# Pooling layer of a two-layer decoder: token scale moved from the tokens to the band matrices, bands built once, first squares split, GpSimd's weight parts in four pieces

## The chip, the cores and the metric

One core of a Trainium2 chip. Its engines run their own instruction queues side by side and wait for each other by semaphores: TensorE (PE in the rows, PEld for its weight loads), VectorE (DVE), ScalarE (ACT), GpSimd (POOL) and SyncE (SP), which here issues all DMAs. The metric is the device time of one launch in microseconds; lower is better.

## The reference

`x` has 512 tokens of 1024 channels, fp32. Layer 0 is a causal pooling mixer and an MLP, layer 1 sliding-window attention and an MLP; each sub-layer has a pre-RMSNorm and a residual, and a final norm follows. The change lies in the pooling mixer:

```
hn = rms_norm(x, g)                      # per token: x * rsqrt(mean(x*x) + eps) * g
for group g, window w in (2, 4, 8, 16):  # 256 channels each
    p_g = mean of hn over the last min(t, w) tokens - hn
y = einsum(p, w_pool) + b                # four 256 x 256 matrices
x = x + y * scale                        # then rms_norm, and the MLP
```

## The kernel before, in words

Activations lie transposed, with 128 channels on the partitions and 512 tokens along the row (eight tiles, `h[c]`). A large matrix product is done as three passes of a rounded 32-bit type: each operand is split in a high part `_h` (ScalarE, a copy that rounds) and a low part `_l` (the difference, on VectorE or GpSimd), and `mm3` (L84 to L86) adds high x high, high x low and low x high in PSUM.

The start of the program, up to about 30 us, is the pooling layer:

- SyncE loads four token tiles `xt` (128 tokens x 1024 channels), then `w_pool`, the small vectors `vec`, the first three weight tiles of the MLP (`wi_raw`, L90), then `h` (the transposed input).
- TensorE does twelve warm-up matmuls (L263) on zeros.
- GpSimd builds eight band matrices of 128 x 144 (L161 to L172): four windows, each once for the first tile (where the mean has fewer tokens) and once for the others. A band column holds 1/w on the tokens of the window, minus 1 on the token itself. A matmul of a token tile against a band gives pooled and transposed channels at once.
- For each token tile ScalarE squares it with a sum per token (L266), a square root, a reciprocal and one Newton step on VectorE give `r0`, VectorE multiplies the whole tile by it (L268, 128 x 1024), and eight fp32 matmuls (L271; each appears as two records) add into eight PSUM banks, one per 128 channels.
- ScalarE and GpSimd split `w_pool` (`wpool_h` L284, `wpool_l` L285). `px_h` (ScalarE, L251) and `px_l` (VectorE, L252) split the pooled banks; after each second one a tile of the MLP's weights is split (`in_weights`, L98 on ScalarE and L99 on GpSimd).
- 48 matmuls of L84 to L86 do the group matrices; `h` gets the result (L305); `f0x_h` and `f0x_l` split it for the MLP, whose first 96 matmuls follow. `n_sq` and `n_acc` (L215, L224 on GpSimd) sum the squares for the next norm, which is applied after these matmuls (L230, L241).

From there on the program is the MLP and the attention layer, with the same splitting. A scheduler puts the instructions of each engine into a fixed order at build time; each engine then works through its own list strictly in that order. The tile pools decide what must wait for a buffer.

## Time and profile before

| | us |
|---|---|
| median of 3 runs | 931.27 |
| the runs | 931.06, 931.27, 932.01 |
| the profiled execution | 932.39 |
| its span | 930.6 |

| engine | busy us | share |
|---|---|---|
| TensorE matmul | 915.2 | 98% |
| VectorE | 574.8 | 62% |
| ScalarE | 427.3 | 46% |
| GpSimd | 135.1 | 15% |

Every row of the trace is from the profiled execution; its times count from the span's start. A row of the timeline gives the start, the length, the engine, the source line and the operation, what it writes and reads, and how many like instructions are merged (x4). In brackets stands how long the engine was idle before it and what it waited for.

### The profile page before, as it was taken

Reading aid. Unit: us, or ns where it says so; the run is one execution under the profiler, and the core shown is the slowest. Engines: PE = TensorE matmul, PEld = TensorE weight load, DVE = VectorE, ACT = ScalarE, POOL = GpSimd, SP = SyncE. Lnnn points to the kernel's source line nnn. Section 1 sums busy time; section 2 is a strip of 40 time slices with the busy share of each in tenths; the row PEclk is TensorE's granted clock in tenths of the full one; section 3 lists DMA queues with packets and bytes.
Section 4 is the critical chain, followed back from the end, with each engine's and each line's share of the span. In section 5 each row is a group of like instructions: output and inputs, shape, how many; then the busy total and the mean of one; then the engine's idle time right before and its main releaser. Section 6 shows DMA issues by size and latency. Waiting matters only on the chain.

```text
span 930.6 us, 11682 instructions
## 1 busy us (share of the span) xinstructions
PE 915.2 (98%) x4419; PEld 771.5 (83%) x4419; DVE 574.8 (62%) x945; ACT 427.3 (46%) x690; POOL 135.1 (15%) x217
## 2 busy tenths in 40 slices
PE   8999999999999999999899999999999999999996
PEld 7788888888888888898788888888888888888896
DVE  5679766335777754456777482987743377777433
ACT  7655443223444443337787451644422244444532
POOL 9600000000000001325654140000000000000022
PEclk9999999999999999999999999999999999999999
DMA  9133222333223223322111041242233422322312
GB/s 333 67 113 113 93 84 80 93 128 113 91 91 105 65 87 106 114 91 68 50 43 46 2 158 39 98 139 104 63 93 100 136 91 91 111 80 63 95 60 91
DMA packets 28855, 88.13 MB, mean 95 GB/s; under 512 B 3200, under 2 KB 4352, under 8 KB 28800
## 3 DMA queue, kind: packets, MB, share of 16 engines
q1 hardware_dynamic: 28800, 87.40, 28.5%
q8 instruction: 34, 0.56, 0.2%
q14 instruction: 21, 0.17, 0.1%
HBM read 85.29 MB, written 2.10 MB: 94 GB/s over the span
## 4 chain that ended last, share of the span: by engine, by line
PE 92%; ACT 3%; DVE 2%; POOL 2%; issue 1%; POOLq 0%; ACTq 0%
PE bank L84 30%; PE bank L85 30%; PE bank L86 30%; PE bank L548 1%; PE bank L578 1%; ACT sc L565 1%; DVE q L464 1%; ACT px_h L251 0%; POOL sc L570 0%; PE bank L241 0%; ACT q_u L457 0%; DVE sc L551 0%; ACT wi_h L98 0%; PE bank L271 0%; ACT th L581 0%
## 5 line engine op out<-in xcount | busy, mean ns | idle before, releaser
L224 POOL TENSOR_TENSOR n_acc<-n_acc,n_sq 128x512 f32<-128x512 f32 (+1 forms) x28 | 39.1, 1395 | 716.4 <-ACT n_sq L215 709.8
L98 ACT ACTIVATE wi_h<-wi_raw 128x1024 fp32r<-128x1024 f32 x88 | 93.0, 1061 | 109.0 <-PE bank L85 100.5
L85 PE MATMUL bank<-f0x_l,wi_h 128*128 128x512 f32 x352 | 137.1, 389 | 0.8 <-DVE f0x_l L252 0.8
L84 PE MATMUL bank<-f0x_h,wi_h 128*128 128x512 f32 x352 | 137.3, 390 | 0.0
L84 PE MATMUL bank<-f1x_h,wi_h 128*128 128x512 f32 x352 | 137.2, 390 | 0.0
L84 PE MATMUL bank<-zh,wo_h 128*128 128x512 f32 (+1 forms) x363 | 137.1, 378 | 0.0
L86 PE MATMUL bank<-f0x_h,wi_l 128*128 128x512 f32 x352 | 137.0, 389 | 0.0
L86 PE MATMUL bank<-f1x_h,wi_l 128*128 128x512 f32 x352 | 137.0, 389 | 0.0
L85 PE MATMUL bank<-f1x_l,wi_h 128*128 128x512 f32 x352 | 137.0, 389 | 0.0
L86 PE MATMUL bank<-zh,wo_l 128*128 128x512 f32 (+1 forms) x363 | 136.6, 376 | 0.0
L85 PE MATMUL bank<-zl,wo_h 128*128 128x512 f32 (+1 forms) x363 | 136.6, 376 | 0.0
L99 DVE TENSOR_TENSOR wi_l<-wi_raw,wi_h 128x1024 fp32r<-128x1024 f32 x84 | 102.6, 1223 | 49.2 <-ACT wi_h L98 37.3
L98 ACT ACTIVATE wo_h<-wo_raw 128x768 fp32r<-128x768 f32 (+1 forms) x70 | 57.5, 823 | 120.2 <-PE bank L85 108.5
L313 DVE TENSOR_TENSOR c_u<-bank,n_rb 128x512 f32<-128x512 f32 x88 | 59.9, 687 | 75.9 <-PE bank L86 75.9
L99 DVE TENSOR_TENSOR wo_l<-wo_raw,wo_h 128x768 fp32r<-128x768 f32 (+1 forms) x66 | 60.3, 914 | 54.4 <-ACT wo_h L98 54.2
L86 PEld LDWEIGHTS bank<-zh,wo_l 128*128 128x128 f32 x363 | 68.3, 188 | 12.5
L84 PEld LDWEIGHTS bank<-zh,wo_h 128*128 128x128 f32 x363 | 68.3, 188 | 12.3
L85 PEld LDWEIGHTS bank<-zl,wo_h 128*128 128x128 f32 x363 | 68.3, 188 | 12.3
L85 PEld LDWEIGHTS bank<-f0x_l,wi_h 128*128 128x128 f32 x352 | 66.1, 188 | 14.6 <-DVE f0x_l L252 1.2
L84 PEld LDWEIGHTS bank<-f0x_h,wi_h 128*128 128x128 f32 x352 | 66.1, 188 | 14.2 <-DVE h L305 0.4
L86 PEld LDWEIGHTS bank<-f1x_h,wi_l 128*128 128x128 f32 x352 | 66.1, 188 | 13.9
L316 ACT ACTIVATE c_t<-c_u,vec 128x512 f32<-128x512 f32 x88 | 70.6, 811 | 15.3 <-DVE c_u L313 14.5
(173 smaller groups left out, 1488.7 us busy)
## 6 DMA issues: line engine op xcount, KB each, us to landing
wi_raw<-w_in SPq DMA_DIRECT2D x88, 512.0 KB, 3.2
wo_raw<-w_out SPq DMA_DIRECT2D x31, 384.0 KB, 3.0
wo_raw<-w_out SPq DMA_DIRECT2D x31, 320.0 KB, 2.8
kq_raw<-w_kq SPq DMA_DIRECT2D x10, 512.0 KB, 3.2
wo_raw<-w_o SPq DMA_DIRECT2D x8, 512.0 KB, 3.2
xt<-x_tok SPq DMA_DIRECT2D x4, 512.0 KB, 5.2
h<-x_t SPq DMA_DIRECT2D x8, 256.0 KB, 7.5
wpool_raw<-w_pool SPq DMA_DIRECT2D x2, 512.0 KB, 8.5
```

The source lines that it names most:

```text
L84: T.matmul(ps, lhsT=wh, rhs=xh, start=start, stop=False, **kw)
L85: T.matmul(ps, lhsT=wh, rhs=xl, start=False, stop=False, **kw)
L86: T.matmul(ps, lhsT=wl, rhs=xh, start=False, stop=stop, **kw)
L98: A.activation(h[:, :n], raw[:, :n], AF.Copy)
L99: (eng or V).tensor_tensor(l[:, :n], raw[:, :n], h[:, :n].bitcast(F32), ALU.subtract)
L224: eng.tensor_tensor(self.acc[:, lo:hi], self.acc[:, lo:hi], sq[:, lo:hi], ALU.add)
L313: V.tensor_tensor(u, ps, rb, ALU.mult)
L316: A.activation(t, u, AF.Identity, bias=col(V_CB + layer * 2 * NF + m), scale=cw[2])
L464: V.tensor_tensor(t[dst], u[src], t[src].bitcast(F32), ALU.subtract)
L548: T.matmul(o, lhsT=qt, rhs=kt[:, kk : kk + 256], start=x == 0, stop=x == 1)
L565: A.activation(t, t, AF.Exp, bias=neg[:, i : i + 1], scale=-1.0, accum_out=den[:, i : i + 1])
L578: T.transpose(ps[:, i * P : (i + 1) * P], sc[i // 2][:, i % 2, kb * P : (kb + 1) * P], ident)
```

## The change

Four bands are built on GpSimd and only the edge part of the other four; VectorE fills the rest by copies, and does the four memsets. The token scale is no longer multiplied into the token tile but into a copy of the band (`sband`, four instructions of 128 x 144 for each tile, two buffers in turn): the matmuls now take the raw tile and the scaled band. The square of the first tile is split in halves, one on ScalarE and one on VectorE, and the sums are added. The low parts that GpSimd makes of the first four MLP weight tiles are made in four instructions of 256 columns instead of one of 1024.

```diff
@@ weights, in_weights
-    def weights(src, n, name, eng=None, raw=None):
+    def weights(src, n, name, eng=None, raw=None, step=1024):
...
         A.activation(h[:, :n], raw[:, :n], AF.Copy)
-        (eng or V).tensor_tensor(l[:, :n], raw[:, :n], h[:, :n].bitcast(F32), ALU.subtract)
+        for a in range(0, n, step):
+            o = slice(a, min(a + step, n))
+            (eng or V).tensor_tensor(l[:, o], raw[:, o], h[:, o].bitcast(F32), ALU.subtract)
         return h, l
...
     def in_weights(layer, j, s, eng=None, raw=None):
-        return weights(w_in[layer, j, s], D, f"wi{layer}_{j}_{s}", eng, raw)
+        return weights(w_in[layer, j, s], D, f"wi{layer}_{j}_{s}", eng, raw, 256 if eng else 1024)
@@ the bands
-    for edge in (True, False):
-        for g, w in enumerate(WINDOWS):
-            b = band[:, 4 * edge + g, :]
-            G.memset(b, 1.0 / w)
-            G.affine_select(b, b, [[1, BW]], ALU.is_ge, 0.0, base=0, channel_multiplier=-1)
-            G.affine_select(b, b, [[-1, BW]], ALU.is_ge, 0.0, base=w - 1, channel_multiplier=1)
-            G.affine_select(b, b, [[1, BW]], ALU.not_equal, 1.0 / w - 1.0, base=0, channel_multiplier=-1)
-            if edge:
-                f = b[:, : w - 1]
-                G.affine_select(f, rc[:, : w - 1], [[1, w - 1]], ALU.is_ge, 0.0, base=0, channel_multiplier=-1)
-                G.tensor_tensor(f, f, ident[:, : w - 1], ALU.subtract)
+    for g, w in enumerate(WINDOWS):
+        b = band[:, g, :]
+        V.memset(b, 1.0 / w)
+        G.affine_select(b, b, [[1, BW]], ALU.is_ge, 0.0, base=0, channel_multiplier=-1)
+        G.affine_select(b, b, [[-1, BW]], ALU.is_ge, 0.0, base=w - 1, channel_multiplier=1)
+        G.affine_select(b, b, [[1, BW]], ALU.not_equal, 1.0 / w - 1.0, base=0, channel_multiplier=-1)
+        f = band[:, 4 + g, : w - 1]
+        G.affine_select(f, rc[:, : w - 1], [[1, w - 1]], ALU.is_ge, 0.0, base=0, channel_multiplier=-1)
+        G.tensor_tensor(f, f, ident[:, : w - 1], ALU.subtract)
+        V.tensor_copy(band[:, 4 + g, w - 1 :], b[:, w - 1 :])
@@ pool_mixer
-        ss0 = small(fst, NT, 32, name="ss0")
+        ss0 = small(fst, 2 * NT, 32, name="ss0")
...
         for i in range(NT):
+            cut = D // 2 if i == 0 else D
             junk = fst.tile([P, D], F32, tag="junk", name=f"junk{i}")
-            A.activation(junk, xt[:, i, :], AF.Square, accum_out=ss0[:, i : i + 1])
+            if cut < D:
+                V.tensor_tensor_reduce(
+                    out=junk[:, cut:], in0=xt[:, i, cut:], in1=xt[:, i, cut:], scale=1.0, scalar=0.0,
+                    op0=ALU.mult, op1=ALU.add, accum_out=ss0[:, NT : NT + 1],
+                )
+            A.activation(junk[:, :cut], xt[:, i, :cut], AF.Square, accum_out=ss0[:, i : i + 1])
+            if cut < D:
+                V.tensor_tensor(ss0[:, i : i + 1], ss0[:, i : i + 1], ss0[:, NT : NT + 1], ALU.add)
             rsqrt_mean(r0[:, i : i + 1], ss0[:, i : i + 1], 1, root=True)
-            V.tensor_scalar(xt[:, i, :], xt[:, i, :], r0[:, i : i + 1], None, ALU.mult)
             n = min(BW, S - i * P)
+            sband = fst.tile([P, 4, BW], F32, tag="sband", name=f"sband{i}", bufs=2)
+            for g in range(4):
+                V.tensor_scalar(sband[:, g, :n], band[:, (0 if i else 4) + g, :n], r0[:, i : i + 1], None, ALU.mult)
             for c in range(NC):
                 T.matmul(
                     banks[c][:, i * P : i * P + n],
                     lhsT=xt[:, i, c * P : (c + 1) * P],
-                    rhs=band[:, (0 if i else 4) + c // 2, :n],
+                    rhs=sband[:, c // 2, :n],
```

The change moves instructions on three engines; rows below are the engines' lists as built, in order, with the semaphores that a row waits for (named by the engine or DMA queue that signals).

VectorE before, from the small chain of the third tile on (L187 v, L188 reciprocal, L200 and L204 the Newton step that ends in r, L268 the scaling of a whole token tile, L297 the bias vector bs, L252 px_l):

```order
L187 TENSOR_SCALAR rs_v<-ss_185 128x1 [waits Activation_49]
L188 RECIPROCAL rs_y<-rs_y 128x1 [waits Activation_49]
L200 SCALAR_TENSOR_TENSOR rs_t<-rs_y,rs_v 128x1 [waits DVE_49]
L204 SCALAR_TENSOR_TENSOR r_184<-rs_t,rs_y 128x1 [waits DVE_49]
L268 TENSOR_SCALAR xt<-xt,r_184 128x1024 [waits DMAHW2_49,DVE_49]
L187 TENSOR_SCALAR rs_v<-ss_185 128x1 [waits Activation_49]
L188 RECIPROCAL rs_y<-rs_y 128x1 [waits Activation_49]
L200 SCALAR_TENSOR_TENSOR rs_t<-rs_y,rs_v 128x1 [waits DVE_49]
L204 SCALAR_TENSOR_TENSOR r_184<-rs_t,rs_y 128x1 [waits DVE_49]
L268 TENSOR_SCALAR xt<-xt,r_184 128x1024 [waits DMAHW3_49,DVE_49]
L297 TENSOR_TENSOR bs<-vec 128x8 [waits DMAHW6_49]
L252 SCALAR_TENSOR_TENSOR px_l<-bank_70,vec,px_h 128x512 [waits Activation_49]
```

VectorE with the change, first from the end of the second tile's chain on (L188, L189, L201 and L205 are v, reciprocal and Newton step; L173 copies the bands, L287 scales them; sband_192 is tile 0's, sband_215 tile 1's):

```order
L205 SCALAR_TENSOR_TENSOR r_164<-rs_t,rs_y 128x1 [waits DVE_49]
L188 TENSOR_SCALAR rs_v<-ss_165 128x1 [waits Activation_49]
L189 RECIPROCAL rs_y<-rs_y 128x1 [waits Activation_49]
L173 COPY band<-band 128x143 [waits Pool_49]
L173 COPY band<-band 128x141 [waits Pool_49]
L287 TENSOR_SCALAR sband_192<-band,r_164 128x144 [waits DVE_49]
L287 TENSOR_SCALAR sband_192<-band,r_164 128x144 [waits DVE_49,Pool_49]
L287 TENSOR_SCALAR sband_215<-band,r_164 128x144
L173 COPY band<-band 128x137 [waits Pool_49]
L173 COPY band<-band 128x129 [waits Pool_49]
```

and then, after tile 0's last two and tile 1's last three scalings, the rows for the tiles 2 (sband_238) and 3 (sband_261):

```order
L201 SCALAR_TENSOR_TENSOR rs_t<-rs_y,rs_v 128x1
L188 TENSOR_SCALAR rs_v<-ss_165 128x1 [waits Activation_49]
L189 RECIPROCAL rs_y<-rs_y 128x1 [waits Activation_49]
L205 SCALAR_TENSOR_TENSOR r_164<-rs_t,rs_y 128x1 [waits DVE_49]
L201 SCALAR_TENSOR_TENSOR rs_t<-rs_y,rs_v 128x1 [waits DVE_49]
L205 SCALAR_TENSOR_TENSOR r_164<-rs_t,rs_y 128x1 [waits DVE_49]
L287 TENSOR_SCALAR sband_238<-band,r_164 128x144 [waits PE_49]
L287 TENSOR_SCALAR sband_238<-band,r_164 128x144 x3
L315 TENSOR_TENSOR bs<-vec 128x8 [waits DMAHW6_49]
L287 TENSOR_SCALAR sband_261<-band,r_164 128x128 [waits DVE_49,PE_49]
L287 TENSOR_SCALAR sband_261<-band,r_164 128x128 x3
L253 SCALAR_TENSOR_TENSOR px_l<-bank_70,vec,px_h 128x512 [waits Activation_49]
```

One long scaling per tile has become four short ones; those of tile 0 stand behind the third tile's v and reciprocal, and those of the tiles 2 and 3 wait for TensorE (for a buffer) and stand ahead of px_l.

GpSimd with the change, from its last band instructions on:

```order
L172 TENSOR_TENSOR band<-band,ident 128x15 [waits Pool_49]
L303 TENSOR_TENSOR wpool_l<-wpool_raw,wpool_h 128x512 [waits DMAHW4_49,Activation_49]
L303 TENSOR_TENSOR wpool_l<-wpool_raw,wpool_h 128x512 [waits Activation_49]
L303 TENSOR_TENSOR wpool_l<-wpool_raw,wpool_h 128x512 [waits DMAHW5_49,Activation_49]
L303 TENSOR_TENSOR wpool_l<-wpool_raw,wpool_h 128x512 [waits Activation_49]
L101 TENSOR_TENSOR wi_0_1_l<-wi_0_1_raw,wi_0_1_h 128x256 [waits DMAHW7_49,Activation_49]
L101 TENSOR_TENSOR wi_0_1_l<-wi_0_1_raw,wi_0_1_h 128x256 x3
```

Before, the same four wpool_l stood there, behind the second half of the bands, and one row of 128x1024 for each wi_l. The fourth weight tile's pieces now also stand ahead of the first n_acc sum instead of behind it, and on ScalarE its high part ahead of the first n_sq. The rest of each engine's list is as before.

## Rows read from the trace of the kernel before

**Rows 1.** The page: busy time, share of the span and instructions of each engine; and the shares of the chain of waits by engine.

```profile
PE 915.2 (98%) x4419; PEld 771.5 (83%) x4419; DVE 574.8 (62%) x945; ACT 427.3 (46%) x690; POOL 135.1 (15%) x217
...
PE 92%; ACT 3%; DVE 2%; POOL 2%; issue 1%; POOLq 0%; ACTq 0%
```

**Rows 2.** The timeline of the first 24 us, all engines.

```profile
7.89 3.18 PE L271 MATMUL bank<-band,xt 128*128 128x144 f32 x24 [1.64 <-DVE rs_y L188]
...
10.96 2.35 ACT L284 ACTIVATE wpool_h<-wpool_raw 128x512 fp32r<-128x512 f32 x4 [0.60 <-DMA wpool_raw<-w_pool]
...
11.40 0.91 DVE L268 TENSOR_SCALAR xt<-xt,r 128x1024 f32<-128x1024 f32 x1
...
12.44 4.96 POOL L285 TENSOR_TENSOR wpool_l<-wpool_raw,wpool_h 128x512 fp32r<-128x512 f32 x4
...
12.52 4.50 PE L271 MATMUL bank<-band,xt 128*128 128x144 f32 x36 [0.35 <-POOL band L168]
...
13.02 0.72 DVE L297 TENSOR_TENSOR bs<-vec 128x8 f32<-128x8 f32 x1 [0.71 <-DMA vec<-vecs]
...
14.32 1.06 ACT L98 ACTIVATE wi_h<-wi_raw 128x1024 fp32r<-128x1024 f32 x1 [1.02 <-DMA wi_raw<-w_in]
...
15.49 2.43 ACT L251 ACTIVATE px_h<-bank,vec 128x512 fp32r<-128x512 f32 x4
...
17.02 0.19 PEld L84 LDWEIGHTS bank<-px_h,wpool_h 128*128 128x128 f32 x1 [0.19 <-DVE px_l L252]
```

**Rows 3.** Timelines around the first stall inside TensorE's run: TensorE, VectorE, ScalarE and GpSimd; the last row is from the chain of waits in order of time (start, length, what) and shows the matmuls that use the sums n_acc.

```profile
29.39 0.39 PE L84 MATMUL bank<-f0x_h,wi_h 128*128 128x512 f32 x1
...
30.60 0.50 PE L85 MATMUL bank<-f0x_l,wi_h 128*128 128x512 f32 x1 [0.82 <-DVE f0x_l L252]
...
31.84 0.39 PE L86 MATMUL bank<-f0x_h,wi_l 128*128 128x512 f32 x1
...
27.80 2.75 DVE L252 SCALAR_TENSOR_TENSOR f0x_l<-h,vec,f0x_h 128x512 fp32r<-128x512 f32 x1 [1.33 <-ACT f0x_h L251]
...
27.03 0.74 ACT L251 ACTIVATE f0x_h<-h,vec 128x512 fp32r<-128x512 f32 x1
...
26.30 1.34 POOL L224 TENSOR_TENSOR n_acc<-n_acc,n_sq 128x512 f32<-128x512 f32 x1 [1.78 <-ACT n_sq L215]
...
27.60 2.40 POOL L99 TENSOR_TENSOR wi_l<-wi_raw,wi_h 128x1024 fp32r<-128x1024 f32 x1
...
38.75 2.98 POOL L224 TENSOR_TENSOR n_acc<-n_acc,n_sq 128x512 f32<-128x512 f32 x2 [0.99 <-ACT n_sq L215]
...
51.29 0.79 PE bank L230 x8
```

**Rows 4.** Sizes. The first two rows are groups by shape in the first 60 us (busy us, mean ns of one); the other three are one line's instructions over the whole span (ns, least/median/most).

```profile
L215 ACT ACTIVATE n_sq<-h 128x512 f32<-128x512 f32 x7 | 4.4, 629 | 0.1
...
L284 ACT ACTIVATE wpool_h<-wpool_raw 128x512 fp32r<-128x512 f32 x4 | 2.3, 622 | 0.7 <-DMA wpool_raw<-w_pool 0.6
...
L551 DVE CUSTOM_DVE_ANT_0 sc<-bank,dist,nsink x64: 340/476/484, 426.2 to 513.3; 128x256 f32<-128x256 f32 x48, 128x128 f32<-128x128 f32 x16
...
L551 DVE DVE_READ_ACCUMULATOR2_ANT neg<- x64: 78/81/88, 426.5 to 513.7; 128x1 f32 x64
...
L266 ACT ACTIVATE junk<-xt x4: 1039/1042/1057, 4.8 to 8.9; 128x1024 f32<-128x1024 f32 x4
```

**Rows 5.** The timeline: the first square root and reciprocal, and the third square root.

```profile
5.96 0.29 ACT L186 ACTIVATE rs_y<-ss,eps 128x1 f32<-128x1 f32 x1
...
6.28 0.16 DVE L188 RECIPROCAL rs_y<-rs_y 128x1 f32<-128x1 f32 x1 [0.17 <-ACT rs_y L186]
...
8.69 0.30 ACT L186 ACTIVATE rs_y<-ss,eps 128x1 f32<-128x1 f32 x1
```

**Rows 6.** The timeline of GpSimd near the end of the program: one instruction with two inputs of 128x256, with nothing beside it.

```profile
918.38 0.74 POOL L680 TENSOR_TENSOR o<-hg,n_rb 128x256 f32<-128x256 f32 x1 [7.11 <-ACT n_rb L244]
```

**Rows 7.** The timeline of VectorE in two narrow windows: the first of four scalings of 128x128 in a row, and the other three merged.

```profile
56.36 0.29 DVE L240 TENSOR_SCALAR n_d<-ident,n_r 128x128 f32<-128x128 f32 x1
...
56.56 0.67 DVE L240 TENSOR_SCALAR n_d<-ident,n_r 128x128 f32<-128x128 f32 x3
```

**Rows 8.** Timelines of GpSimd and VectorE at two places. First a scaling from SBUF to SBUF (L437) that starts beside a subtraction on GpSimd, and the next one, alone; then three f0x_l in a row with the sums n_acc beside them (each row one instruction; a start may lie before the end of the one ahead).

```profile
408.71 2.42 POOL L99 TENSOR_TENSOR kq_l<-kq_raw,kq_h 128x1024 fp32r<-128x1024 f32 x1 [9.85 <-ACT kq_h L98]
...
410.47 0.94 DVE L437 TENSOR_SCALAR ku<-ku,vec 128x512 f32<-128x512 f32 x1
...
411.33 0.47 DVE L437 TENSOR_SCALAR ku<-ku,vec 128x512 f32<-128x512 f32 x1
...
32.45 0.73 DVE L252 SCALAR_TENSOR_TENSOR f0x_l<-h,vec,f0x_h 128x512 fp32r<-128x512 f32 x1
...
32.63 1.71 POOL L224 TENSOR_TENSOR n_acc<-n_acc,n_sq 128x512 f32<-128x512 f32 x1 [0.94 <-ACT n_sq L215]
...
33.14 1.76 DVE L252 SCALAR_TENSOR_TENSOR f0x_l<-h,vec,f0x_h 128x512 fp32r<-128x512 f32 x1
...
34.82 1.79 DVE L252 SCALAR_TENSOR_TENSOR f0x_l<-h,vec,f0x_h 128x512 fp32r<-128x512 f32 x1
```

**Rows 9.** TensorE by stages: the stage, its length, busy time (instructions), the granted clock as a share of full speed, DMA share, GB/s.

```profile
448.80:451.60 2.80, 0.00 (x0) 1.00 0.56 187
...
452.20:455.60 3.40, 3.40 (x14) 0.50 0.39 143
```

More of the change, by code (lines that the diff above doesn't have):

```diff
@@ L264, in pool_mixer @@
         for i in range(NT):
+            cut = D // 2 if i == 0 else D
             junk = fst.tile([P, D], F32, tag="junk", name=f"junk{i}")
-            A.activation(junk, xt[:, i, :], AF.Square, accum_out=ss0[:, i : i + 1])
+            if cut < D:
+                V.tensor_tensor_reduce(
+                    out=junk[:, cut:],
+                    in0=xt[:, i, cut:],
+                    in1=xt[:, i, cut:],
+                    scale=1.0,
+                    scalar=0.0,
+                    op0=ALU.mult,
+                    op1=ALU.add,
+                    accum_out=ss0[:, NT : NT + 1],
+                )
+            A.activation(junk[:, :cut], xt[:, i, :cut], AF.Square, accum_out=ss0[:, i : i + 1])
+            if cut < D:
+                V.tensor_tensor(ss0[:, i : i + 1], ss0[:, i : i + 1], ss0[:, NT : NT + 1], ALU.add)
             rsqrt_mean(r0[:, i : i + 1], ss0[:, i : i + 1], 1, root=True)
-            V.tensor_scalar(xt[:, i, :], xt[:, i, :], r0[:, i : i + 1], None, ALU.mult)
             n = min(BW, S - i * P)
+            sband = fst.tile([P, 4, BW], F32, tag="sband", name=f"sband{i}", bufs=2)
+            for g in range(4):
+                V.tensor_scalar(sband[:, g, :n], band[:, (0 if i else 4) + g, :n], r0[:, i : i + 1], None, ALU.mult)
             for c in range(NC):
```

## The prediction

> **What bounds it now.** The page first: TensorE is busy 98% of the span, and the chain of waits lies on it for 92% [rows 1]. So a change in the first 25 us pays only as far as it moves the moment at which TensorE starts its unbroken run, or takes out a stall inside that run. The timeline of the first 24 us gives that moment: the first L84 matmul at 17.02 [rows 2]. It follows the last pooling matmul without a gap and waits 0.19 us for px_l. Two chains arrive there together: the pooling matmuls (64 records, 7.89 to 17.02, with holes where they wait for bands), and ScalarE, which needs the wi_raw transfer until 14.32, converts it until 15.38 and only then may do px_h at 15.49. ScalarE alone allows px_h at about 15.40, so nothing that speeds up pooling can bring L84 forward by more than 0.1 us.
>
> Inside the run I looked at each place where TensorE waits. The first is at 29.39 [rows 3]: the matmuls stand 0.23 us apart, but the next starts at 30.60, and from 29.39 to 31.84 five steps take 2.45 us where 5 x 0.23 = 1.15 would do: 1.3 us lost. TensorE waits for a f0x_l that took 2.75 us on VectorE (one in rows 8 took 0.73). Beside it GpSimd's subtraction wi_l runs from 27.60 to 30.00, and f0x_l ends 0.55 after it: it was held until GpSimd was through.
>
> **Pieces of wi_l.** Four 128x256 subtractions take the place of 128x1024. A GpSimd instruction of 128x256 takes 0.74 [rows 6], so f0x_l is held by at most 0.74 instead of 2.2. In the old positions f0x_h ends at 27.77; with one hold and its own 0.55 to 0.73, f0x_l ends at 29.1 to 29.3, and TensorE wants it at 29.62. The stall goes: -1.3. Bounds: 0 (all of it stays) and -1.3 (there is no more to gain). The pieces add 4 x 0.74 - 2.40, about 0.5 us per weight, which GpSimd's idle 1.78 us before 26.30 covers [rows 3]. In ScalarE's order n_sq moves behind a weight conversion, so the n_acc sums end up to 1.1 later than 41.73; they are wanted at 51.29 [rows 3]. Nothing.
>
> **First squares on two engines.** The half square takes 0.63 on ScalarE (n_sq has that size) instead of 1.04. VectorE's half, an instruction with sums like L551's, lies between 0.48 (128x256) and 1.04 (ScalarE's whole row); with L551's 0.136 for each further 128 columns it is 0.75 [rows 4]. With 0.08 to read the sum out and 0.16 (a tiny instruction, rows 5) to add the halves that is 0.99, where ScalarE's whole row took 1.04 and its read-out some 0.1 more: the first square root starts 0.15 earlier, at 5.8 instead of 5.96. Each later square follows on ScalarE, so the third square root, too, ends 0.15 earlier, at 8.84 [rows 5].
>
> **The order on VectorE is what counts.** In the listing of the change the four tile-0 scalings no longer follow tile 0's r. Ahead of them stand both chains of tile 1 and the v and reciprocal of tile 2, which needs that third square root; then two copies. With a start every 0.2 us for such small instructions [rows 7], reciprocal at 8.87, two copies, first scaling until about 9.65: TensorE gets its first pooling matmul at 9.7, not 7.89. It starts 1.8 us later, and gets rid of the holes. Pooling alone costs 48 records x 0.1225 + 16 x 0.109 = 7.6 us (the 36 records from 12.52, without a hole, took 4.5: 20 of 144 columns, 16 of 128, and the last one's tail) [rows 2]. From 9.7 that gives the last tile's first column at 15.6, px_h at 16.1 (0.52 after it, as before), and L84 1.53 after px_h: 17.6. By this alone the start is 0.6 late. The four memsets that move to VectorE delay the warm-up matmuls by at most 4 x 0.18; TensorE's wait for 9.7 covers that.
>
> **GpSimd is free too early.** Band building on GpSimd shrinks from 24 selects and 8 memsets to 12 selects. With 12 left of 32 instructions of full width, what ended at 12.44 is done some microseconds before 11.58. Then it waits for wpool_h: 10.96 + 0.62 = 11.58, where ScalarE itself waited for the transfer [rows 2, 4]. So the four wpool_l subtractions start at 11.58 instead of 12.44, and then four pieces of wi_l (ready at 15.38) follow without a gap. Before, VectorE's last large scaling ended at 12.31, ahead of them. After, the scalings of tiles 2 and 3 come into just this stretch, because their two buffers are free only when TensorE has done tile 0 (9.7 + 2.0 = 11.7) and tile 1 (13.6).
>
> What does a scaling cost there? Three rows. A scaling from SBUF to SBUF of 128x512 (L437) took 0.47 alone and 0.94 when a GpSimd subtraction was running; it ended 0.28 after that one's end [rows 8]. The tiny bs, 128x8, took 0.72 beside wpool_l [rows 2]; a tiny instruction takes 0.16 [rows 5]. And when both engines have a queue, they take turns: f0x_l 0.73, n_acc 1.71 (1.34 in rows 3), f0x_l 1.76, and after another n_acc f0x_l 1.79 [rows 8], although VectorE's next instruction stood ready each time. The Trainium skill ("SBUF — State Buffer", Who interferes with whom) says that a VectorE instruction in a two-port mode, such as a tensor_scalar, and a GpSimd instruction shut each other out for a whole instruction; it does not say who goes next when both wait. By that rule alone these eight scalings would cost between two holds and eight. The rows of f0x_l say eight.
>
> So, by turns: GpSimd's queue is 4 x 1.2 + 4 x 0.66 (0.62 to 0.74), and after each of the eight VectorE gets in one instruction of about 0.1. That ends at 11.58 + 7.4 + 0.8 = 19.8. VectorE has nine to place: four scalings of tile 2, bs, four of tile 3. The first of tile 3 comes after the sixth hold, at 18.3, and the last at 20.05. Behind it in VectorE's queue stands px_l (0.7): L84 at 20.9. If the three small r instructions just ahead also fall after 11.58 (I get 11.55 for the first), there are twelve to place: the eight turns are used up by bs, tile 3's scalings run freely to 20.7, its first column is done by 20.4, px_h at 20.7 and px_l end at 22.1: L84 at 22.2. I take 21.5: +4.5. Bounds: -0.1 (ScalarE's limit) and +5.2 (GpSimd runs out of work and must wait for ScalarE's next wi_h). The later px and f0x chains on ScalarE move with it (3.4 to 5.2), so the first term's argument holds.
>
> **Sum.** +4.5 - 1.3 = +3.2. TensorE's work after L84 is the same in the same order, so this reaches the end. The profiled execution had 932.39 for a span of 930.6; the median of the runs is 931.27, 1.1 less. On the median: 931.27 + 3.2 = 934.5. From L84 at 20.9 to 22.2, and 0.6 to 1.3 for the stall, the case itself spans 933.5 to 935.9.
>
> **Rivals.** *No turns (not slower).* VectorE keeps going once it is in: the four scalings of a tile then cost one hold. Tile 2's would run from 12.8 to 13.4, before TensorE wants them (13.6), tile 3's are as easily hidden, and L84 stands at 17.6: +0.6 - 1.3 = -0.7, 930.6. For it speaks that no row shows several one-source scalings in a row against a GpSimd queue. Against it: f0x_l and n_acc. It decides at the second scaling of tile 2: if that starts 0.2 after the first, this is the case.
>
> *TensorE's clock.* After 2.8 us of idling (448.8 to 451.6) its granted clock was 0.50, the 1.2 GHz level, from 452.2 to 455.6 [rows 9]: 3.4 us at half speed cost 1.7. Now it will idle from about 6.9 (the memsets move the warm-up's end by up to 0.7) to 9.7, also 2.8, where it was 1.64 before 7.89 [rows 2]. If half speed comes in tiles 0 and 1, the holds cover it. If it falls on the first matmuls after L84, because TensorE works only a third of the time from 13 to 21, it is +1.7: 936.2. Together with no turns: 932.3.
>
> *The stall stays.* If f0x_l finds a new piece in front each time, it is still one instruction, so one hold; I give this little. It would be 935.8.
>
> *Faster.* L84 at 16.9 with the stall gone is -1.4, 929.9; it needs the first scalings near 7, which the order rules out. More than 0.2% needs 929.4.
>
> **Numbers.** Turns with the full clock 0.55, turns with half clock at L84 0.14, turns with the stall left or only part of the holds 0.09, no turns 0.15, no turns with half clock 0.04, faster still 0.03. Without the no-turns cases the range would leave out 0.22 and the edges, so it goes down to them: 930.4 to 937.0. A measurement here tells 0.2% (1.9 us) from no change. Slower by more: the turns cases but a rest, 0.73; within: no turns and that rest, 0.22; faster by more: 0.05, some of it from a run in which the half-clock stretch at 452 does not come.
>
> **What the next profile should show.** First pooling matmul near 9.7; wpool_l from 11.6; the first eight scalings 0.3 each, those of tiles 2 and 3 mostly 0.7 to 1.3 each with a GpSimd subtraction beside them; px_h near 19 to 20.7; L84 near 21.5; then no gap near f0x_l, which takes under 1.5. It is wrong if the scalings of tile 2 start 0.2 apart, if L84 stands before 19, or if the gap at f0x_l is still over 0.5.

## The result and the profile after

| | before | after |
|---|---|---|
| median, us | 931.16 (4 runs) | 935.79 (4 runs) |
| the runs, us | 931.03 to 932.01 | 935.32 to 936.45 |
| profiled execution, us | 932.39 | 935.32 |
| its span, us | 930.6 | 933.6 |

The change makes the kernel 0.45% slower: the ratio is 1.0045, with a 95% interval of 1.0032 to 1.0057. The forecast was 934.5. In the later comparisons the kernel before has medians of 932.23 to 932.29 (10 to 27 runs), and beside those the change is 3.5 us longer.

The page still shows TensorE busy for 98% of the span and the chain of waits on it for 92%, as in [rows 1]:

```profile
PE 917.5 (98%) x4419; PEld 774.4 (83%) x4419; DVE 579.5 (62%) x968; ACT 427.0 (46%) x690; POOL 131.0 (14%) x209
...
PE 92%; ACT 3%; DVE 3%; DMA 1%; issue 1%; POOL 0%; SPq 0%; ACTq 0%; POOLq 0%; DVEq 0%
```

So the loss is again a matter of the first 25 us. TensorE's timeline there, to compare with the first and the last row of [rows 2]:

```profile
1.80 5.93 PE L264 MATMUL bank<-warm 128*128 128x144 f32 x24 [1.80 <-DVE warm L262]
9.98 6.53 PE L289 MATMUL bank<-sband,xt 128*128 128x144 f32 x36 [2.25 <-DVE sband L287]
16.98 2.13 PE L289 MATMUL bank<-sband,xt 128*128 128x144 f32 x12 [0.46 <-DVE sband L287]
19.70 2.05 PE L289 MATMUL bank<-sband,xt 128*128 128x128 f32 x16 [0.60 <-DVE sband L287]
21.76 0.50 PE L84 MATMUL bank<-px_h,wpool_h 128*128 128x512 f32 x1
```

The pooling starts at 9.98 (7.89 before), and the unbroken run at 21.76 (17.02 before): 4.74 later. Why, the chain of waits in order of time says (start, length, what): from 11.96 to 19.66 it lies on VectorE, with two tiny instructions of the Newton step, tile 2's first scaling (its time is put down as issue) and the three others, bs, and the first scaling of tile 3. None of these eight waits for TensorE.

```profile
11.96 1.22 DVE rs_t L201
13.20 1.19 DVE r L205
14.45 1.18 issue
15.62 2.67 DVE sband L287 x3
18.29 0.61 DVE bs L315
18.90 0.76 DVE sband L287
19.70 2.05 PE bank L289 x16
```

Beside them, GpSimd's timeline, which has no hole between 11.87 and 19.56, and two single rows of VectorE from narrow windows: the last scaling ahead of GpSimd's start, and the first one within it.

```profile
11.87 4.95 POOL L303 TENSOR_TENSOR wpool_l<-wpool_raw,wpool_h 128x512 fp32r<-128x512 f32 x4 [5.00 <-ACT wpool_h L302]
16.78 2.78 POOL L101 TENSOR_TENSOR wi_l<-wi_raw,wi_h 128x256 fp32r<-128x256 f32 x4
...
11.34 0.29 DVE L287 TENSOR_SCALAR sband<-band,r 128x144 f32<-128x144 f32 x1
...
14.31 1.39 DVE L287 TENSOR_SCALAR sband<-band,r 128x144 f32<-128x144 f32 x1
```

The same instruction takes 0.29 us alone and 1.39 when four subtractions of 1.24 stand in GpSimd's queue; once the pieces are up, it takes 0.76 to 0.82. The engines take turns, one instruction each: VectorE's eight from 11.96 to 19.66 stand beside GpSimd's eight from 11.87 to 19.56.

The stall of [rows 3] is gone. Its f0x_l (2.75 us before) now takes 0.91 beside the same weight's pieces:

```profile
32.54 0.91 DVE L253 SCALAR_TENSOR_TENSOR f0x_l<-h,vec,f0x_h 128x512 fp32r<-128x512 f32 x1 [1.32 <-ACT f0x_h L252]
...
31.45 3.29 POOL L101 TENSOR_TENSOR wi_l<-wi_raw,wi_h 128x256 fp32r<-128x256 f32 x4 [2.14 <-ACT wi_h L98]
```

The matmuls that use the sums n_acc, in TensorE's timeline before and after:

```profile
51.13 0.95 PE L230 MATMUL bank<-ones,n_acc 128*128 128x2 f32 x8
```

```profile
54.53 0.95 PE L231 MATMUL bank<-ones,n_acc 128*128 128x2 f32 x8
```

They start 3.4 later (the chain in [rows 3] has 51.29 for the first; the marks below are the timeline's): of the 4.74, the pieces gave back 1.3. From there to the end little changes (span +3.0).

TensorE's first pooling row holds one thing more. By stages (length, busy time, ..., granted clock third from the end), 16 of the 32 records of tiles 0 and 1 ran at a granted clock of 0.50, the 1.2 GHz level:

```profile
9.98:10.80 0.82, 0.81 (x6) 0.82 (x7) 0.82 (x6) 0.61 (x3) 0.00 (x0) 1.00 0.98 388
10.80:14.10 3.30, 3.30 (x16) 3.30 (x15) 3.27 (x11) 2.30 (x4) 2.23 (x2) 0.50 1.04 421
```

### The profile page after: what moved, and what is told of

Same layout as the page of the kernel before. It is cut to its first block, busy times and chain, and to the rows that moved or that the text cites. A ratio compares the mean times of both kernels' runs of the same rounds, so it can differ in the third digit from the quotient of the medians.

```text
span 933.6 us, 11695 instructions
## 1 busy us (share of the span) xinstructions
PE 917.5 (98%) x4419; PEld 774.4 (83%) x4419; DVE 579.5 (62%) x968; ACT 427.0 (46%) x690; POOL 131.0 (14%) x209
## 4 chain that ended last, share of the span: by engine, by line
PE 92%; ACT 3%; DVE 3%; DMA 1%; issue 1%; POOL 0%; SPq 0%; ACTq 0%; POOLq 0%; DVEq 0%
PE bank L84 30%; PE bank L86 30%; PE bank L85 29%; PE bank L566 1%; ACT sc L583 1%; PE bank L596 1%; DMA xt<-x_tok 1%; DVE q L482 1%; DVE sband L287 1%; ACT q_u L475 1%; ACT q L481 0%; DVE tl L600 0%; DVE sc L569 0%; ACT th L599 0%; POOL sc L588 0%
## 5 line engine op out<-in xcount | busy, mean ns | idle before, releaser
L84 PE MATMUL bank<-f1x_h,wi_h 128*128 128x512 f32 x352 | 137.1, 390 | 0.0
L84 PE MATMUL bank<-f0x_h,wi_h 128*128 128x512 f32 x352 | 137.1, 390 | 0.0
L84 PE MATMUL bank<-zh,wo_h 128*128 128x512 f32 (+1 forms) x363 | 137.0, 378 | 0.0
L101 DVE TENSOR_TENSOR wo_l<-wo_raw,wo_h 128x768 fp32r<-128x768 f32 (+1 forms) x66 | 60.4, 915 | 54.5 <-ACT wo_h L98 54.3
L84 PEld LDWEIGHTS bank<-zh,wo_h 128*128 128x128 f32 x363 | 68.3, 188 | 12.3
L85 PEld LDWEIGHTS bank<-f1x_l,wi_h 128*128 128x128 f32 x352 | 66.1, 188 | 13.7
```

What stands on the lines that cost most here:

```text
L84: T.matmul(ps, lhsT=wh, rhs=xh, start=start, stop=False, **kw)
L85: T.matmul(ps, lhsT=wh, rhs=xl, start=False, stop=False, **kw)
L101: (eng or V).tensor_tensor(l[:, o], raw[:, o], h[:, o].bitcast(F32), ALU.subtract)
```

## The experiments

Ten kernels were run. The executions of one kernel lie 1 to 3 us apart as a rule (up to 6 in e8), so for effects of that size the marks in the trace say more than the medians. One table holds the marks: the first pooling matmul, the idle time ahead of it and the clock from 10.8 to 14.1 us; the first mixer matmul (L84 of the change); the first matmul on n_acc; the span.

| kernel | pooling | idle | clock | mixer | n_acc | span |
|---|---|---|---|---|---|---|
| before | 7.89 | 1.64 | 1.00 | 17.02 | 51.1 | 930.6 |
| the change | 9.98 | 2.25 | 0.50 | 21.76 | 54.5 | 933.6 |
| e1, before with pieces | 7.89 | 2.10 | 1.00 | 17.02 | 49.9 | 929.1 |
| e4, change without pieces | 9.41 | 2.01 | 0.58 | 22.32 | 55.6 | 935.1 |
| e3, change without wpool_l | 9.70 | 2.17 | 0.54 | 19.30 | 52.1 | 931.6 |
| e2, scale on the tokens | 9.43 | 1.85 | 0.53 | 19.03 | 51.8 | 929.8 |
| e10, wpool_l in halves | 9.83 | 2.32 | 0.55 | 20.91 | 53.7 | 932.9 |
| e6, order tile by tile | 7.04 | 0.44 | 1.00 | 17.38 | 50.2 | 929.8 |
| e7, e2 with a longer warm-up | 9.47 | 0.78 | 1.00 | 17.44 | 50.2 | 929.6 |
| e8, change with a longer warm-up | 9.24 | 1.78 | 1.00 | 20.51 | 53.3 | 932.9 |
| e5, before with pieces everywhere | 7.14 | 0.58 | 1.00 | 17.28 | 50.1 | 927.4 |
| e9, put together | 7.45 | 0.15 | 1.00 | 15.38 | 48.9 | 926.3 |

### The pieces: e1 and e4

e1 puts only the new loop of `weights` and its 256 columns into the kernel before; e4 takes them out of the change:

```diff
-        return weights(w_in[layer, j, s], D, f"wi{layer}_{j}_{s}", eng, raw, 256 if eng else 1024)
+        return weights(w_in[layer, j, s], D, f"wi{layer}_{j}_{s}", eng, raw, 1024)
```

> The kernel before with one edit: GpSimd's low parts of the first four MLP weights in pieces of 256 columns. Holds theory: the start of TensorE's run stays at 17.0 us (first L84-form matmul), f0x_l takes under 1.5 us instead of 2.75, the gap at 29.4 us is gone, and the statistics matmuls that stood at 51.3 stand at 50.0: 1.3 us less, 0.14%. Rival (the pieces do nothing, f0x_l is late for another reason): gap and 51.3 stay, no change.

> The changed kernel with the low parts of the MLP weights undivided again (128x1024). Holds theory: GpSimd's work in the stretch is the same in sum, so L84 stands within 0.7 us of 21.8; the fourth weight's subtraction holds f0x_l again for up to 2.4 us and TensorE loses up to 1.3 us near 33 us: 0.5 to 2 us over the change. Rival (the pieces themselves make the start late, by giving GpSimd more turns): L84 more than 1.5 us earlier, time under the change.

e1 took 930.80 us beside 932.23 for before, ratio 0.9985 (0.9976 to 0.9994). The mixer starts at the same 17.02, and n_acc is used 1.28 us earlier (49.85 for 51.13): the -1.3 of the stall, alone. e4 took 936.88, ratio 1.0059 (1.0040 to 1.0077), and its span is 1.5 longer than the change's. Its trace shows what the pieces cost and bring within the change. VectorE and TensorE of e4:

```profile
15.81 2.45 DVE L287 TENSOR_SCALAR sband<-band,r 128x144 f32<-128x144 f32 x1
...
18.31 4.01 PE L289 MATMUL bank<-sband,xt 128*128 128x144 f32 x32 [3.04 <-DVE sband L287]
...
33.10 1.88 DVE L253 SCALAR_TENSOR_TENSOR f0x_l<-h,vec,f0x_h 128x512 fp32r<-128x512 f32 x1 [1.32 <-ACT f0x_h L252]
```

The undivided subtraction holds one scaling, the first of tile 2, for 2.45 us, and then VectorE runs freely, where with pieces nearly every instruction is held for a short time. But so the first band of tile 2 comes only at 18.3, and TensorE has tiles 2 and 3 in one go still to do: the mixer starts 0.56 later than with pieces, and f0x_l is held again (1.88). Part of the 0.56 may be chance: GpSimd began 1.06 earlier in this execution, at 10.81, and held all four Newton instructions of tiles 2 and 3, two in the change.

### The turns: e3, e2, e10

e3 leaves out GpSimd's four wpool_l (the mixer uses wpool_h in their place, so the low part is missing from its sums); e2 scales the tokens again, four instructions in place of sixteen; e10 cuts wpool_l in two:

```diff
@@ e3
-            G.tensor_tensor(ll, raw, hh.bitcast(F32), ALU.subtract)
-            wpool.append((hh, ll))
+            wpool.append((hh, hh))
@@ e2
+            V.tensor_scalar(xt[:, i, :], xt[:, i, :], r0[:, i : i + 1], None, ALU.mult)
-            sband = fst.tile([P, 4, BW], F32, tag="sband", name=f"sband{i}", bufs=2)
-            for g in range(4):
-                V.tensor_scalar(sband[:, g, :n], band[:, (0 if i else 4) + g, :n], r0[:, i : i + 1], None, ALU.mult)
...
-                    rhs=sband[:, c // 2, :n],
+                    rhs=band[:, (0 if i else 4) + c // 2, :n],
@@ e10
-            G.tensor_tensor(ll, raw, hh.bitcast(F32), ALU.subtract)
+            for k in range(2):
+                o = slice(k * 256, k * 256 + 256)
+                G.tensor_tensor(ll[:, o], raw[:, o], hh[:, o].bitcast(F32), ALU.subtract)
```

> The changed kernel without GpSimd's four wpool_l instructions: the low part of the pooling matrices is not computed, the high part is used in its place, with the same matmuls. VectorE's order is that of the change. Holds theory: nothing holds the scalings of tile 2 (0.3 us each), those of tile 3 meet at most the pieces of wi_l after 15.6; TensorE does its pooling from 10.0 without waiting for a band, with 1.6 us lost to the half clock: L84 at about 19.6, 2.2 us earlier than with the change. Rival (late start and clock alone): L84 at 21.8 as before this edit.

> The changed kernel with the token scale back on the token tiles (one 128x1024 instruction per tile); bands, copies, half squares and pieces as changed. Holds theory: the eight scalings that took turns with GpSimd are gone, but the copies still stand behind the third reciprocal, so pooling starts at about 9.5 and the half-clock stretch (1.6 us) is no longer hidden: L84 at about 19, against 21.8 with the change and 17.0 before; the f0x_l gap is gone. Total 2.8 us under the change, about 0.5 us over before. Rival (the late start and the clock alone make the change late, the turns are hidden behind them): L84 stays near 21.8.

> The change with the four subtractions for wpool_l cut into two of 256 columns each; nothing else. Theory (each two-input instruction and each scaling on VectorE lets one subtraction of GpSimd pass, so its length is what one turn costs): beside them the scalings of tiles 2 and 3 and the instructions of the root take 0.6 to 0.8 us, not 1.2 to 1.4; five to seven turns at 0.55 less each, the first mixer matmul at 18.5 to 19.5 in place of 21.76 (there TensorE at the half clock is the bound), and the time 2 to 3 us under the change, 933. Rival (the delay belongs to GpSimd's work as a whole, or to the scalings themselves): the instructions still take 1.2 us or more, and the mixer starts at 21.3 or later.

e3 took 933.18, ratio 1.0010 (1.0000 to 1.0019). VectorE in tile 2, with nothing on GpSimd, and TensorE:

```profile
13.31 0.91 DVE L287 TENSOR_SCALAR sband<-band,r 128x144 f32<-128x144 f32 x4 [1.25 <-PE bank L289]
...
9.70 9.60 PE L289 MATMUL bank<-sband,xt 128*128 128x144 f32 x64 [2.17 <-DVE sband L287]
```

Four scalings take 0.91 us, not 3.98 as in the change, and wait only for TensorE to give back a buffer; TensorE runs through its 64 records without a hole. The turns are the cause of the holes, and the mixer starts 2.46 us earlier without them (2.2 were expected). It is 2.3 later than before all the same: 64 records need 9.60 us, where e7 below needs 7.97. That is the half clock, and here nothing covers it.

e2 took 932.81, ratio 1.000 (0.999 to 1.001), and starts the mixer at 19.03 with the same 9.60 us of pooling: sixteen scalings or four, without turns TensorE's clock sets the end.

e10 took 934.78, ratio 1.0027 (1.0015 to 1.0039). A turn does get cheaper with the size of GpSimd's instruction, as expected; VectorE's single rows in e10:

```profile
11.88 0.69 DVE L201 SCALAR_TENSOR_TENSOR rs_t<-rs_y,rs_v 128x1 f32<-128x1 f32 x1
...
12.49 0.14 DVE L188 TENSOR_SCALAR rs_v<-ss 128x1 f32<-128x1 f32 x1
...
12.63 0.63 DVE L205 SCALAR_TENSOR_TENSOR r<-rs_t,rs_y 128x1 f32<-128x1 f32 x1
...
14.55 0.84 DVE L287 TENSOR_SCALAR sband<-band,r 128x144 f32<-128x144 f32 x1
```

Among them the tiny L188, with one input, takes 0.14 us as if it were alone; the two Newton instructions, as tiny but with two inputs, are held. Yet the mixer starts at 20.91, where I had expected 18.5 to 19.5. I had kept the number of turns and halved the price. But GpSimd has no less to do (5.60 + 2.78 us for wpool_l and the first wi_l, 4.95 + 2.78 in the change), only in more turns, and VectorE pays for nearly all of them: eleven of its instructions, up to tile 3's first scaling, stand beside GpSimd's twelve, eight beside eight in the change. How much of the 0.85 us won at the mixer is due to the pieces, the run does not tell: GpSimd began 0.8 earlier in this execution, at 11.07, and that alone put more of VectorE's instructions beside it. In both kernels VectorE's long queue pays for nearly all of GpSimd's work in the stretch, 7.6 us here and 7.7 in the change; the size of a piece counts where VectorE has a single instruction to place, as f0x_l in e1.

### The order: e6

e6 gives each tile a buffer of its own and holds the next tile's root behind the scalings of the tile ahead, so that tile 0's scalings no longer stand behind the third tile's reciprocal; bs goes behind the last scaling:

```diff
-            rsqrt_mean(r0[:, i : i + 1], ss0[:, i : i + 1], 1, root=True)
-            sband = fst.tile([P, 4, BW], F32, tag="sband", name=f"sband{i}", bufs=2)
+            sband = fst.tile([P, 4, BW], F32, tag="sband", name=f"sband{i}", bufs=4)
+            with tc.issue_after(last.ins) if last else nullcontext():
+                rsqrt_mean(r0[:, i : i + 1], ss0[:, i : i + 1], 1, root=True)
             for g in range(4):
-                V.tensor_scalar(sband[:, g, :n], band[:, (0 if i else 4) + g, :n], r0[:, i : i + 1], None, ALU.mult)
+                last = V.tensor_scalar(sband[:, g, :n], band[:, (0 if i else 4) + g, :n], r0[:, i : i + 1], None, ALU.mult)
```

> The change, with VectorE's order set tile by tile: each tile's reciprocal root, then its four scalings, then the next tile's root; a buffer for each tile's scaled bands; the work for bs behind the last scaling. Theory (the late first matmul is VectorE's order alone; the rest is turns with GpSimd): the first pooling matmul starts at 7.7 to 8.0 us in place of 9.98, TensorE's clock isn't halved between 10.8 and 14.1, and only tile 3's root and scalings still take turns with the four subtractions for wpool_l, so that the first mixer matmul (L84 in the change) starts at 18.5 to 20 us in place of 21.76; the time is 2 to 3 us under the change, within 1.3 us of before. Rival 1 (all of the loss is the order): it starts at 17.1 and the time is 1.3 us under before. Rival 2 (scaled bands are late for another reason, such as the building of the bands): the first pooling matmul stays near 9.5 and the mixer above 21.

It took 932.44, ratio 1.0007 (0.9998 to 1.0015): 3.3 us under the change, a little more than expected. TensorE and VectorE in e6:

```profile
7.04 7.04 PE L291 MATMUL bank<-sband,xt 128*128 128x144 f32 x56 [0.44 <-DVE sband L289]
14.32 0.71 PE L291 MATMUL bank<-sband,xt 128*128 128x128 f32 x4 [0.24 <-DVE sband L289]
15.56 0.71 PE L291 MATMUL bank<-sband,xt 128*128 128x128 f32 x4 [0.52 <-DVE sband L289]
17.38 0.50 PE L84 MATMUL bank<-px_h,wpool_h 128*128 128x512 f32 x1 [1.11 <-DVE px_l L253]
...
11.34 0.16 DVE L205 SCALAR_TENSOR_TENSOR r<-rs_t,rs_y 128x1 f32<-128x1 f32 x1
11.54 3.96 DVE L289 TENSOR_SCALAR sband<-band,r 128x128 f32<-128x128 f32 x4
15.42 1.24 DVE L318 TENSOR_TENSOR bs<-vec 128x8 f32<-128x8 f32 x1
```

The pooling starts at 7.04, ahead of the expected 7.7 to 8.0, since the first token tile landed early: its square began at 4.21, at 4.87 in the change. The order is what counts all the same, for in e8 below, which has the change's order, the square began at 4.22 and the pooling at 9.24.

The mixer's 17.38 is nearer to the first rival's 17.1 than to my 18.5 to 20. I had counted tile 3's root among the turns, but in this execution it ended at 11.50, just ahead of GpSimd's start at 11.68; only the four scalings (3.96) and bs (1.24) still take turns, and TensorE is busy with other tiles for most of that. (The third root came at 8.53 instead of 8.96; how much of the margin is due to that, the run does not tell.) The turns that are left are not free: TensorE waits 1.11 us for px_l, which stands behind these scalings and behind bs, where my edit had put it. So most of the loss lies in the order in which the change leaves VectorE's queue: it makes the pooling late, and puts the scalings beside GpSimd's queue. Which of the three parts of the edit (order, buffers, bs) does how much, the run does not tell. By the span e6 is 0.8 under before; the medians show no difference.

### The clock: e7 and e8

e7 is e2, and e8 the change, with one more edit:

```diff
-        for i in range(12):
+        for i in range(16):
             T.matmul(banks[-1][:, :BW], lhsT=warm[:, :P], rhs=warm, start=True, stop=True)
```

> The change with the token's scale back on the tokens (as in the run before that did this), and with 16 warm-up matmuls in place of 12, so that TensorE idles at most 1 us, not 1.9, ahead of the first pooling matmul. Theory (the half clock from 10.8 to 14.1 us is the answer to the idle stretch in front of the pooling, and costs there what it takes away, since nothing else holds the pooling matmuls in that kernel): no half clock, and the first mixer matmul starts at 17.4 to 17.8 in place of 19.0; the time falls by 1.2 to 1.6. Rival (the half clock comes of what TensorE does from 10 us on): half clock as before, mixer at 19.0 or later, the time the same.

> The change with 16 warm-up matmuls in place of 12 and nothing else. It asks whether the half clock over tiles 0 and 1 costs the change anything. The prediction's theory (covered: TensorE waits for tile 2's and tile 3's scaled bands anyway): full clock from 10 us on, more idle time of TensorE ahead of tiles 2 and 3 (some 1.5 us more than the 1.06 us now), and the first mixer matmul still at 21.3 to 21.8; the time within 0.3 us of the change. Rival (the scalings of tiles 2 and 3 wait in their turn for TensorE to give back the two buffers of scaled bands, so the half clock is passed on): the mixer at 20.2 to 20.6, the time 1.2 to 1.6 us under the change.

TensorE's timeline of the pooling in e2 and the row of the stage (the granted clock third from the end), and then the same two views of e7:

```profile
9.43 9.60 PE L287 MATMUL bank<-band,xt 128*128 128x144 f32 x64 [1.85 <-DVE band L173]
```

```profile
10.80:14.10 3.30, 3.30 (x16) 3.30 (x16) 3.19 (x6) 2.24 (x5) 2.82 (x3) 0.53 1.03 418
```

```profile
9.47 7.97 PE L287 MATMUL bank<-band,xt 128*128 128x144 f32 x64 [0.78 <-DVE band L173]
17.44 0.50 PE L84 MATMUL bank<-px_h,wpool_h 128*128 128x512 f32 x1
```

```profile
10.80:14.10 3.30, 3.30 (x29) 3.30 (x28) 3.19 (x7) 1.84 (x4) 3.05 (x3) 1.00 1.02 411
```

The pooling starts at the same moment and ends 1.6 us earlier; in 3.3 us it does 29 records instead of 16. The mixer's 17.44 is the theory's 17.4 to 17.8. In time the gain is not shown: e7 took 931.49 where e2 took 932.81, but the ratios are 0.9997 (0.9988 to 1.0005) and 1.000 (0.999 to 1.001), and in the profiled executions e2 makes up for it later (last section). Whether every execution of e2 has the half clock, its one profile does not tell.

e8 took 935.40, ratio 1.0046 (1.0027 to 1.0064): in time, the change's own 1.0045. The half clock is gone, TensorE waits longer ahead of tiles 2 and 3 (2.07 us, 1.06 in the change), and nothing is won. Its mixer starts 1.25 earlier than the change's, where the theory had 21.3 to 21.8, and that seems to speak for the rival. But in this execution the third root came 0.74 earlier (8.22), so that three of the four Newton instructions of tiles 2 and 3 were ahead of GpSimd's start, two in the change; and its scalings of tile 2 follow each other with no wait for TensorE. The time alone does not settle it, since a gain of 1.2 us would just lie within e8's interval. The change's own chain does: from 11.96 to 19.66 VectorE never waits for TensorE to give back a buffer, and its scaling at the end of that stretch sets TensorE's start on tile 3. So there the half clock was not passed on; it was covered.

### The same subtraction elsewhere, and the sum: e5 and e9

e5 is before with every low part that GpSimd makes cut into 256 columns, also those of the attention's weights. e9 is the change with the scale on the tokens, the root of each tile pinned behind the scaling and the copies ahead of it, pieces everywhere, and on ScalarE two px_h ahead of the first wi_h:

```diff
@@ e5 and e9, weights
+        step = 256 if eng is G else 1024
+        for a in range(0, n, step):
@@ e9, pool_mixer
+            with ExitStack() as pins:
+                if last:
+                    pins.enter_context(tc.issue_after(last.ins))
+                    pins.enter_context(tc.issue_after(copied[1 if i == 1 else 3].ins))
+                rsqrt_mean(r0[:, i : i + 1], ss0[:, i : i + 1], 1, root=True)
+            last = V.tensor_scalar(xt[:, i, :], xt[:, i, :], r0[:, i : i + 1], None, ALU.mult)
...
-                ws.append(in_weights(0, *pre[c // 2], G, raws[c // 2]))
+                with tc.issue_after(heads[-1].ins):
+                    ws.append(in_weights(0, *pre[c // 2], G, raws[c // 2]))
```

> The kernel before, with every low part that GpSimd makes of a weight cut into pieces of 256 columns: those of the first feed-forward layer, and those of the attention's weights as well. Theory (a subtraction of 128x1024 on GpSimd holds VectorE's two-input instructions for its whole length, so pieces shorten what VectorE waits): the 1.3 us of the pieces in the first layer come here too, and TensorE's longest wait, 2.9 us for q at the start of the attention, shrinks, by up to 2 us where q stands behind a whole subtraction; the half clock that follows this wait in most runs (some 3.3 us of it, 1.6 us lost) then stays away. Between 1.3 and 5 us faster than before, 927 to 930.5. Rival (the wait for q belongs to VectorE's own work or to a chain in front of it): the wait stays at 2.9 us, and the time is that of the run with pieces in the first layer alone, 1.3 to 1.4 us under before.

> What the runs so far point to, put together: the change's half-built bands and copies, the token's scale on the tokens, VectorE's order set tile by tile (root, scaling, two copies, next tile), pieces of 256 columns in every low part of a weight on GpSimd, and on ScalarE the first two px_h ahead of the first wi_h. Theory: the pooling starts at 7.0 to 7.4 and runs without a gap at the full clock for 8.0 us; px_h starts at 14.3 to 14.7 in place of 15.5, the first mixer matmul at 15.9 to 16.5 in place of 17.0 before; the wait for q in the attention is as short as in the run with pieces everywhere (longest 1.1 us), with no half clock behind it. With that run's 929.0 less 0.6 to 1.1: 927.9 to 928.5, 0.4 per cent under before. Rival (ScalarE or the mixer's weights are late next, since wi_h comes later): TensorE waits for wi_l or f0x near 27 us, and the time is 929.0 or above.

e5 took 929.02, ratio 0.9972 (0.9963 to 0.9982). At the start of the attention, VectorE and GpSimd before, then VectorE, GpSimd and TensorE in e5:

```profile
448.85 3.45 DVE L464 TENSOR_TENSOR q<-q_u,q 64x512 fp32r<-64x512 f32 x2 [2.09 <-ACT q L463]
...
446.34 4.70 POOL L99 TENSOR_TENSOR kq_l<-kq_raw,kq_h 128x1024 fp32r<-128x1024 f32 x2 [0.19 <-ACT kq_h L98]
```

```profile
447.86 2.09 DVE L467 TENSOR_TENSOR q<-q_u,q 64x512 fp32r<-64x512 f32 x2 [2.08 <-ACT q L466]
...
445.44 6.50 POOL L102 TENSOR_TENSOR kq_l<-kq_raw,kq_h 128x256 fp32r<-128x256 f32 x8
...
448.86 0.39 PE L551 MATMUL bank<-kh,q 128*128 128x256 f32 x1 [1.09 <-DVE q L467]
450.00 0.39 PE L551 MATMUL bank<-kh,q 128*128 128x256 f32 x1 [0.41 <-DVE q L467]
```

The wait of 2.9 us splits into 1.09 and 0.41, and the half clock of [rows 9] does not follow. e9 took 928.09, ratio 0.9960 (0.9947 to 0.9972), the fastest kernel here. TensorE and ScalarE in e9:

```profile
7.45 7.93 PE L294 MATMUL bank<-band,xt 128*128 128x144 f32 x64
15.38 0.50 PE L84 MATMUL bank<-px_h,wpool_h 128*128 128x512 f32 x1
...
13.85 1.26 ACT L254 ACTIVATE px_h<-bank,vec 128x512 fp32r<-128x512 f32 x2 [0.57 <-PE bank L294]
15.01 1.06 ACT L98 ACTIVATE wi_h<-wi_raw 128x1024 fp32r<-128x1024 f32 x1
```

The mixer starts 1.64 us ahead of before and 1.9 ahead of e5 (I had expected 15.9 to 16.5); of the 1.9, 1.2 is left at n_acc and 1.1 in the span. With the change's half-built bands no hole is left in the pooling, and px_h no longer stands behind wi_h; the run does not part the two.

## Why the prediction came out right

The forecast was +3.2; the span grew by 3.0 and the median by 4.6. The agreement of the spans is partly luck, for the profiled execution of before (932.39) lies above all four of its runs, and that of the change (935.32) is as fast as the fastest of its four; beside the later medians of before it is 3.5. The mechanism shows in the marks: +4.74 at the mixer, for a forecast of +4.5, and +3.4 at n_acc. (In the prediction's sum for the case itself, 20.9 and the full 1.3 give 933.85 as its lower end, not 933.5; nothing hangs on it.) The single steps:

- **The stall goes, -1.3.** Right: 1.28 in e1, and 1.34 in the change (4.74 at the mixer, 3.4 at n_acc).
- **Half squares, 0.15 earlier.** Mis-sized. From the start of the first square to the first root it takes 1.08 us, 1.18 before: 0.10 won, but the token tile came 0.09 later, and the root stands at 5.95. In the nine kernels with half squares this stretch is 1.04 to 1.21, in the three without 1.18 to 1.19. The third root stands at 8.96, where 8.69 was before: ScalarE waits for the token tile at the third square, so a term of ScalarE's own work was counted where the transfer is what ends last. No run had the half squares alone.

```profile
7.78 1.06 ACT L280 ACTIVATE junk<-xt 128x1024 f32<-128x1024 f32 x1 [0.16 <-DMA xt<-x_tok]
...
8.96 0.29 ACT L187 ACTIVATE rs_y<-ss,eps 128x1 f32<-128x1 f32 x1
```

- **The order makes the first pooling matmul late, 9.7.** Right, 9.98; the 0.28 more comes from that root, which ended at 9.25 and not at 8.84. e6 shows that it is the order: with another one 7.04, and 9.24 with this one in e8, where the first tile landed at the same time.
- **By that alone, the mixer at 17.6.** Right only at the full clock: 17.44 in e7. With the half clock that the profiled executions of e2 and e3 show, it is 19.0 to 19.3.
- **Turns, the mixer at 21.5.** Right, 21.76. GpSimd started at 11.87 and was through at 19.56 (11.58 and 19.8 were forecast). The 21.5 was a choice between nine instructions to place (20.9) and twelve (22.2); the trace has eleven, with two of the small r instructions behind GpSimd's start, and eight of them paid a hold, as forecast. The rule for the turns that was read from [rows 8], one instruction each way, holds for scalings as for f0x_l: the second scaling of tile 2 starts 1.31 us after the first, not the 0.2 that would have been the sign of no turns. The Trainium skill ("SBUF — State Buffer", Who interferes with whom) also says that a VectorE instruction with two inputs in SBUF contends with a GpSimd instruction that reads SBUF. The traces agree, down to 128x1, which took 1.19 to 1.23 here.
- **The holds cover the half clock in tiles 0 and 1.** Borne out by the change's own chain, in which VectorE waits for TensorE nowhere between 11.96 and 19.66; the time of e8 agrees, its marks leave it open.
- **The rival without turns, 930.6.** Its mechanism was run in e2 and e3, and its mixer at 17.6 was wrong: it starts at 19.03 and 19.30. The term that failed there is the clock, to which the prediction gave a fifth of that case's chance: without the holds the half clock costs 1.6 us in tiles 0 and 1 (9.60 us of pooling where e7 has 7.97), and it came in both. In time the forecast was -0.7 beside before, or +1.0 with the half clock; e3's ratio of 1.0010 (1.0000 to 1.0019) fits the second, e2's 1.000 (0.999 to 1.001) does not decide.

The two losses therefore do not add up. Taking away the turns alone wins 2.5 us at the mixer (e3), a longer warm-up alone nothing in time, with 1.25 at the mixer that an earlier root explains (e8), and both together 4.3 (e7).

## What to carry over

Before an instruction is given to VectorE, look at what GpSimd does at that time: beside a full GpSimd queue, each scaling of 128x144 and each two-input instruction, down to 128x1, cost a whole GpSimd instruction here, and a long VectorE queue paid for nearly all of GpSimd's work. Cut GpSimd's instructions into pieces where a single VectorE instruction on the critical path stands behind them; where there are many, look for an order that moves one of the two queues out of the other's way, as in e6. And look at the order that the scheduler makes of independent small chains: here a first tile's work stood behind a third tile's root, and the kernel with a pinned order, e6, won back nearly all of the loss.

## What was not expected of the hardware

- The idle time ahead of the pooling does not by itself decide the clock. After 2.10 us without work in e1, 1.64 before and 1.78 in e8 the clock stayed full; after 1.85 in e2, 2.01 in e4 and 2.17 in e3 it was 0.53 to 0.58 from 10.8 to 14.1, the half rate for most of that time. What TensorE did before parts the twelve profiles better. In the five kernels that lost the clock (the change, e2, e3, e4, e10) it still went through the warm-up at 6 records per us from 5 to 6 us. In before, e1, e6 and e8 it had reached 9 to 11 records per us by then. In e5, e7 and e9 it had not, but the pooling followed the warm-up within 0.8 us. The moment differs between kernels that do the same until then (the change, e6, e8), and in e8 it came before the four added matmuls. So whether another execution of the change has the half clock at all, its profile does not tell. This is a pattern in twelve single executions; what decides is open. TensorE from 5 to 6 us in the change, then in e8 (busy time, records, granted clock; the clock reads 1.00 in both, so for the warm-up it is the records that tell the pace):

```profile
5.00:6.00 1.00, 1.00 (x6) 1.00 0.91 356
```

```profile
5.00:6.00 1.00, 1.00 (x11) 1.00 1.00 389
```

- The half clock in the attention is not there in every execution. In e2's, the same wait of 2.9 us was followed by the full clock, and the span from n_acc to the end is 878.0 us, where it is 879.1 to 879.6 in nine of the others (879.5 before); in e5 and e9, with the shorter waits, it is 877.3 and 877.4. Single executions of one kernel differ by that much.

The stage that follows e2's wait (clock third from the end):

```profile
452.60:456.00 3.40, 3.40 (x21) 2.80 (x21) 3.37 (x14) 1.37 (x6) 0.20 (x1) 1.00 0.41 154
```

- The first token tile's square began between 4.08 us (e5) and 4.87 us (the change), although the same transfers are issued at the same place. So marks of two single executions can differ by 0.8 us without any change in the program.
